# A two-layer hybrid encoder: softmax sums applied to a pair of heads' result, and five smaller moves around attention

## The chip, the cores and the metric

The kernel runs on one core of a Trainium2 chip. The metric is the device time of one execution in microseconds (us). The core's engines run side by side, each through its own list of instructions in order: TensorE (PE; its weight loads are listed as PEld), VectorE (DVE), ScalarE (ACT), GpSimd (POOL) and SyncE (SP), which only issues transfers. POOL and ACT can issue transfers too.

## The reference

Two layers on x of 512 x 1024, each a feed-forward half step, a mixer, and another feed-forward half step. All inputs are float32. The mixer, cut to what matters here:

```python
proj = h @ w_in
qa, ka, va, ub, qc, kc, vc, f_lin, g_lin = split(proj)
ya = chunked_relpos_attention(qa, ka, va, qk_gain[0], qk_gain[1], rel_bias)   # 8 heads of 64
yb = multiscale_pool(ub, w_pool, pool_scale)
yc = forgetting_attention(qc, kc, vc, qk_gain[2], qk_gain[3], f_lin + forget_bias)
branch = einsum('bsnw,nwd->bsnd', stack([ya, yb, yc]), w_branch)
merged = sum(sigmoid(g_lin) * branch)
return merged @ w_out

# in both attentions, with q and k normalised per head (rms_norm):
logits = q @ k.T + bias          # a: bias by relative distance; c: cq - ck, the cumulated log gates
p = softmax(where(mask, logits, -1e30))
out = p @ v
```

## The kernel before

Every product is made of three float32r products, hi x hi, hi x lo and lo x hi (`triple`, lines 119 to 121). For that each operand is split into a high and a low half: weights in `wchunk` (line 271 on ACT makes `whi`, line 273 on DVE makes `wlo`), other data in `split_to` (lines 378 and 379). Weights stream in on SP's queue.

The program is written to a scheduler that puts each engine's instructions in order by a model of its own. On top of it the code keeps a counter, `pe[0]`, of the matmul work issued so far in units of one 512-column matmul. `later(delay, fn)` defers a piece of work until the counter has gone on by `delay`: a row block's transposes come LAG_T = 24 units after its logits, a head's value products LAG_V = 14 units after the transposes. Between the heads, `attention` draws work from a generator, the filler, so that PE has projections or merge products to do while the other engines work through a softmax.

A mixer goes through these stages: the projections of q and k for attention "a" (`proj_qk` 0 and 1) and of v (`proj_v` 2); attention "a" over eight heads, with the projections for attention "c" (3, 4, 5) and the forgetting gates (`forget`) as filler; attention "c" over eight heads, with the first merge (`merge_units` of `ya`) as filler; then pooling, the other merges and the output product. In layer 0 the two attentions lie at about 465 to 700 us, in layer 1 at about 1690 to 1900 us.

One row block (128 queries) of one head in `attention`: logits on PE (L951, L952), the bias strip added and the row maximum taken on DVE (L955), Exp with its row sum on ACT (L959), the reciprocal of the sum on DVE (L961), the probabilities scaled by it (L962, on POOL for the first three blocks and on DVE for the fourth), transposes on PE (L974), which ACT and DVE copy out of PSUM as a high and a low half (L978, L979). A half of a head's value products (L996, L997) goes to a PSUM tile `o`. ACT copies one half of it (L1000), DVE adds the other (L1001), and ACT and POOL split the 64 x 256 result into a pair's rows `y` (L378, L379). A pair is two heads, 128 rows. `merge_units` reads the pair's rows as right operand k of its products.

PSUM has eight banks: four under the name `acc` (projections and merges) and four under `mm` (logits, transposes, value products, the turning of q and k). A projection's evacuation copies the bank to `ptb` (L826), squares the bank's content (L828) and sums the squares (L829). The first projection of a mixer starts from normalised data that comes in two halves of 256 tokens (`norm.back`), with three weight chunks loaded ahead (`pre`) and the fourth loaded after both halves. The turning of q and k (L844 to L859) is deferred in steps set by TURN.

Of the kernel before, what the change touches and what calls it, by code (L numbers as in the profile page):

```python
# [40 lines left out]
def encoder_kernel(tc, xT, c, w_ada, b_ada, gains, w_gate, w_up, w_down, w_qkv, w_f, w_ubg,  # L41
# [130 lines left out]

    x_dram = dr.tile([4, P, 2 * T], F32, name="x_dram")
    fv_dram = [dr.tile([H, FVLEN], F32, name=f"fv_dram{l}") for l in range(L)]

    last = {}

# [591 lines left out]
    def proj(l, col, evac, pre=None, norm=None):  # L769
        accs = [acc() for _ in range(NT)]  # L770

        def three(t, k, hi, lo):
            tk = slice(t * P, (t + 1) * P)
            triple2(accs[t], hhi[:, k, tk], hlo[:, k, tk], hi, lo, k == 0, k == KD - 1)

        if norm is not None:
            for hs in range(2):
                norm.back(hs, mmt)
                if hs == 0:
                    later(FRONT2, lambda: norm.front(1, mmt))  # L780
                    later(BACK2, lambda: norm.back(1, mmt))
                for k in range(6):
                    hi, lo = pre[k // 2]
                    for t in (2 * hs, 2 * hs + 1):
                        three(t, k, hi[:, k % 2, :], lo[:, k % 2, :])
        else:
            for c in range(2):
                hi, lo = qkv_chunk(l, col, c)
                for kk in range(2):
                    for t in range(NT):  # L790
                        three(t, 2 * c + kk, hi[:, kk, :], lo[:, kk, :])
                        yield
        held = [(c, *qkv_chunk(l, col, c)) for c in ((3,) if pre else (2, 3))]
        for t in range(NT):
            for c, hi, lo in held:
                for kk in range(2):
                    three(t, 2 * c + kk, hi[:, kk, :], lo[:, kk, :])
                    yield
            evac(t, accs[t])
# [18 lines left out]
    def proj_qk(l, col, gcol, is_q, res, pre=None, norm=None):  # L818
# [3 lines left out]
        def evac(t, a):  # L822
# [2 lines left out]
            qn, ss = qs  # L825
            nc.scalar.copy(qn[:, t, :], a)  # L826
            sq = t2(T)
            nc.scalar.activation(sq, a, AF.Square)  # L828
            nc.vector.tensor_reduce(ss[:, t, :], sq.rearrange("p (h d) -> p h d", h=H), axis=AX.X, op=ALU.add)  # L829

        yield from proj(l, col, evac, pre, norm)
# [44 lines left out]

    turns = []
    heads = [H]
    TURN = 52
    Q_GATE, K_GATE = (2, 2, 4, 4), (6, 6, 8, 8)  # L880

    def finish_turns(upto=3):
# [57 lines left out]
    def attention(qs, ks, vs, strip, ys, filler, budget, group):  # L940


        open_pt = {}

        def logits(h, i, strips):
            p, off = divmod(h, 2)
# [8 lines left out]
            nc.vector.tensor_tensor_reduce(out=lg, in0=s[:, :n], in1=strips[i], scale=-1.0, scalar=BIG,  # L955
                                           op0=ALU.add, op1=ALU.min, accum_out=mx)
            pr = t2(T)[:, :n]
            sm = st([P, 1], F32, "sm", 4)
            nc.scalar.activation(pr, lg, AF.Exp, bias=mx, scale=-1.0, accum_out=sm)  # L959
            rs = st([P, 1], F32, "rs", 4)  # L960
            nc.vector.reciprocal(rs, sm)  # L961
            (nc.vector if i == NT - 1 else nc.gpsimd).tensor_scalar(pr, pr, rs, None, op0=ALU.mult)  # L962
            pe[0] += 0.5 * (i + 1.5)
            later(LAG_T, lambda: turn(h, i, pr), group)

# [18 lines left out]
        def weigh(h, half, pt):  # L984
# [1 line left out]
            rows = slice(off * HD, off * HD + HD)  # L986
            other = slice(HD - off * HD, 2 * HD - off * HD)
            if off == 0 and half == 0:
                ys.append(blk("b"))
            y = ys[p]  # L990
            o = mmt((P, HALF))
            nj = 2 * half + 2
            for j in range(nj):
                q0 = P if j == nj - 1 else 0
# [3 lines left out]
            cols = slice(half * HALF, (half + 1) * HALF)  # L998
            yl = t1(T)[:, :HALF]
            nc.scalar.copy(yl[rows, :], o[other, :])  # L1000
            nc.vector.tensor_tensor(yl[rows, :], o[rows, :], yl[rows, :], op=ALU.add)  # L1001
            split_to(y[rows, 0, cols], y[rows, 1, cols], yl[rows, :], nc.gpsimd)
            pe[0] += 1.0 * nj

        for h in range(H):
            strips = strip(h)
# [13 lines left out]
            for _ in filler:  # L1020
                pass

    LAG_T, LAG_V = 24, 14


    def pool_front(l, g):
# [77 lines left out]
    class Mixer:  # L1104
# [10 lines left out]
        def run(self, nxt):  # L1115
# [14 lines left out]
            def fill_a():  # L1130
                yield from proj_qk(l, 3, g8[:, 2:3], True, qc)
                yield from proj_qk(l, 4, g[:, 3:4], False, kc)
                yield from proj_v(l, 5, "v2", vc)
                yield from forget(l)

            lo_share[0] = LO_SHARE
            attention(qa, ka, va, lambda h: strip_a(l, h), ya, fill_a(), FILL_A, "a")
# [133 lines left out]
```

## Time and profile before

| what | value |
|---|---|
| median of 3 runs | 2451.54 us (2450.65 to 2452.75) |
| profiled execution | 2450.88 us |
| its span | 2448.9 us |
| granted TensorE clock, mean | 0.998 |
| DMA packets, bytes | 116279, 320.23 MB |

The span is the time from the first to the last recorded instruction; 2.0 us of the execution lie outside it. In the rows of the profile, "mm L974 <- POOL t L962" under the waits means that line 974 with its output `mm` waited until POOL's line 962 had written `t`; names carry no buffer numbers. `t` stands for the work tiles `t1` and `t2`, `b` for the tiles of 128 x 1024 that hold y and q.

### The profile page before, as it was taken

How to read it: one execution, taken by the hardware profiler on the slowest of the kernel's cores; microseconds unless marked ns; L12 is line 12 of the kernel's file. 1: busy time of each engine (PE TensorE's matmuls, PEld its weight loads, DVE VectorE, ACT ScalarE, POOL GpSimd, SP SyncE). 2: the span in 40 equal slices, each digit the busy share in tenths (PEclk: the TensorE clock that was granted, in tenths of full speed). 3: DMA queues.
4: the chain of work that ended last, by engine and by line, in shares of the span. 5: the costliest groups of instructions: out<-in, count | busy, mean ns of one | idle time of the engine just before them, and what ended most of it. 6: DMA issues, size and time to landing. Idle time of an engine off the chain costs nothing. (4 is left out here: it accounts for less than half of the span.)

```text
span 2448.9 us, 34028 instructions
## 1 busy us (share of the span) xinstructions
PE 2396.8 (98%) x12966; PEld 2051.8 (84%) x12966; DVE 1600.5 (65%) x2859; ACT 1110.3 (45%) x1888; POOL 377.3 (15%) x439
## 2 busy tenths in 40 slices
PE   7999999999999999999999999999999999999999
PEld 5798888777888898988898888878777888988888
DVE  8978766677643378787678656477765434765463
ACT  5333345677642353333453334366765333533341
POOL 3000002144532110000000000123354322000000
PEclk9999999999999999999999999999999999999999
DMA  7756543222323426565327423223133234233232
GB/s 284 251 170 209 198 147 113 78 82 88 116 91 103 142 75 240 174 206 198 129 85 243 138 86 121 103 90 96 61 109 99 95 111 139 87 104 112 67 114 78
DMA packets 116279, 320.23 MB, mean 131 GB/s; under 512 B 11122, under 2 KB 13298, under 8 KB 116116
## 3 DMA queue, kind: packets, MB, share of 16 engines
q1 hardware_dynamic: 114962, 313.86, 38.3%
q0 software_dynamic: 1152, 4.19, 0.4%
q8 instruction: 102, 1.67, 0.3%
q14 instruction: 61, 0.50, 0.1%
q10 hardware_dynamic: 2, 0.00, 0.0%
HBM read 311.64 MB, written 6.38 MB: 130 GB/s over the span
## 5 line engine op out<-in xcount | busy, mean ns | idle before, releaser
L271 ACT CAST whi<-raw 128x1024 fp32r<-128x1024 f32 (+1 forms) x325 | 338.2, 1044 | 595.1 <-PE mm L120 289.2
L273 DVE TENSOR_TENSOR wlo<-raw,whi 128x1024 fp32r<-128x1024 f32 x317 | 392.2, 1240 | 197.4 <-ACT whi L271 194.2
L121 PE MATMUL mm<-hhi,wlo 128*128 128x512 f32 x744 | 289.8, 390 | 0.7 <-DVE wlo L273 0.4
L119 PE MATMUL mm<-hhi,whi 128*128 128x512 f32 x744 | 290.2, 390 | 0.0
L120 PE MATMUL mm<-hlo,whi 128*128 128x512 f32 x744 | 290.0, 390 | 0.0
L119 PE MATMUL acc<-b,whi 128*128 128x512 f32 (+1 forms) x704 | 264.1, 376 | 1.7 <-ACT b L378 1.7
L121 PE MATMUL acc<-b,wlo 128*128 128x512 f32 (+1 forms) x704 | 262.1, 374 | 3.5 <-DVE wlo L273 3.5
L120 PE MATMUL acc<-b,whi 128*128 128x512 f32 (+1 forms) x704 | 262.4, 373 | 0.0
L197 DVE CUSTOM_DVE_ANT_0 v<-v,b,badac 128x1024 f32<-128x1024 f32 x144 | 188.3, 1316 | 60.9 <-DMA v<-in_w_ada_dram 60.7
L119 PE MATMUL acc<-hhi,whi 128*128 128x512 f32 x480 | 190.7, 399 | 1.7 <-ACT hhi L738 1.7
L121 PE MATMUL acc<-hhi,wlo 128*128 128x512 f32 x480 | 188.9, 394 | 0.0
L120 PE MATMUL acc<-hlo,whi 128*128 128x512 f32 x480 | 188.5, 393 | 0.2 <-DVE hlo L741 0.2
L121 PEld LDWEIGHTS mm<-hhi,wlo 128*128 128x128 f32 x744 | 139.7, 188 | 30.9 <-DVE wlo L273 1.6
L119 PEld LDWEIGHTS mm<-hhi,whi 128*128 128x128 f32 x744 | 140.0, 188 | 27.9
L120 PEld LDWEIGHTS mm<-hlo,whi 128*128 128x128 f32 x744 | 139.7, 188 | 27.4
L121 PEld LDWEIGHTS acc<-b,wlo 128*128 128x128 f32 x704 | 133.8, 190 | 27.2 <-DVE wlo L273 4.6
L119 PEld LDWEIGHTS acc<-b,whi 128*128 128x128 f32 x704 | 133.3, 190 | 23.8 <-ACT b L378 2.6
L120 PEld LDWEIGHTS acc<-b,whi 128*128 128x128 f32 x704 | 133.3, 189 | 23.2 <-DVE b L379 0.9
L119 PE MATMUL acc<-whi,hhi 128*128 128x512 f32 x336 | 137.7, 411 | 4.4 <-ACT t L828 3.7
L120 PE MATMUL mm<-b,whi 128*128 128x512 f32 (+1 forms) x384 | 135.8, 354 | 0.0
L119 PE MATMUL mm<-b,whi 128*128 128x512 f32 (+1 forms) x384 | 135.8, 354 | 0.0
L121 PE MATMUL mm<-b,wlo 128*128 128x512 f32 (+1 forms) x384 | 135.6, 354 | 0.0
(300 smaller groups left out, 5598.3 us busy)
## 6 DMA issues: line engine op xcount, KB each, us to landing
v<-in_w_ada_dram SPq DMA_DIRECT2D x144, 512.0 KB, 4.4
raw<-in_w_down_dram SPq DMA_DIRECT2D x88, 512.0 KB, 3.5
raw<-in_w_up_dram SPq DMA_DIRECT2D x82, 512.0 KB, 3.4
b<-in_w_gate_dram SPq DMA_DIRECT2D x76, 512.0 KB, 5.3
raw<-in_w_ubg_dram SPq DMA_DIRECT2D x56, 512.0 KB, 3.3
raw<-in_w_qkv_dram SPq DMA_DIRECT2D x42, 512.0 KB, 3.7
raw<-in_w_branch_dram SPq DMA_DIRECT2D x24, 512.0 KB, 3.6
raw<-in_w_out_dram SPq DMA_DIRECT2D x16, 512.0 KB, 3.3
```

Source lines behind the costliest of these rows:

```text
L119: mm(o, lh, rh, start=start, stop=False, skip_group_check=onto)
L120: mm(o, lh, rl, start=False, stop=False, skip_group_check=onto)
L121: mm(o, ll, rh, start=False, stop=stop, skip_group_check=onto)
L197: dot = nc.vector.tensor_tensor_reduce(out=raw, in0=raw, in1=silc[0], scale=1.0, scalar=badac[:, l, j, d:d + 1], op0=ALU.mult, op1=ALU.add ...
L271: nc.scalar.copy(hi, raw)
L273: lo_eng.tensor_tensor(lo, raw, hi.bitcast(F32), op=ALU.subtract)
```

## The change

- The reciprocal and the scaling of each row block go. The row sums of a pair (two heads, four blocks each) are gathered in a tile of 128 x 8, one reciprocal is taken for the pair, and a transfer on POOL's queue writes it to `inv_dram` as 1024 single floats. A new `norm_rows`, LAG_N = 8 units after the pair's last value product, reads them back as two broadcast transfers of 64 x 512 on POOL's queue; DVE multiplies the pair's unscaled 128 x 512 rows by them, and ACT and DVE split the result. The splits by quarter (64 x 256, ACT and POOL) go.
- The Square of a projection reads the copy in SBUF in place of the PSUM bank.
- The value products of attention "c" go to an `acc` bank.
- `forget` stands ahead of `proj_v` 5 in the filler.
- The first projection loads its fourth weight chunk after its first half, and finishes two of four token blocks in each half.
- TURN is 60 in place of 52.

```diff
@@ -172,6 +172,7 @@
 
     x_dram = dr.tile([4, P, 2 * T], F32, name="x_dram")
     fv_dram = [dr.tile([H, FVLEN], F32, name=f"fv_dram{l}") for l in range(L)]
+    inv_dram = {(g, p): dr.tile([2, T], F32, name=f"inv_dram_{g}{p}") for g in "ac" for p in range(4)}
 
     last = {}
 
@@ -783,6 +784,13 @@
                     hi, lo = pre[k // 2]
                     for t in (2 * hs, 2 * hs + 1):
                         three(t, k, hi[:, k % 2, :], lo[:, k % 2, :])
+                if hs == 0:
+                    end = qkv_chunk(l, col, 3)
+                for t in (2 * hs, 2 * hs + 1):
+                    for kk in range(2):
+                        three(t, 6 + kk, end[0][:, kk, :], end[1][:, kk, :])
+                    evac(t, accs[t])
+            return
         else:
             for c in range(2):
                 hi, lo = qkv_chunk(l, col, c)
@@ -790,7 +798,7 @@
                     for t in range(NT):
                         three(t, 2 * c + kk, hi[:, kk, :], lo[:, kk, :])
                         yield
-        held = [(c, *qkv_chunk(l, col, c)) for c in ((3,) if pre else (2, 3))]
+        held = [(c, *qkv_chunk(l, col, c)) for c in (2, 3)]
         for t in range(NT):
             for c, hi, lo in held:
                 for kk in range(2):
@@ -825,7 +833,7 @@
             qn, ss = qs
             nc.scalar.copy(qn[:, t, :], a)
             sq = t2(T)
-            nc.scalar.activation(sq, a, AF.Square)
+            nc.scalar.activation(sq, qn[:, t, :], AF.Square)
             nc.vector.tensor_reduce(ss[:, t, :], sq.rearrange("p (h d) -> p h d", h=H), axis=AX.X, op=ALU.add)
 
         yield from proj(l, col, evac, pre, norm)
@@ -876,7 +884,7 @@
 
     turns = []
     heads = [H]
-    TURN = 52
+    TURN = 60
     Q_GATE, K_GATE = (2, 2, 4, 4), (6, 6, 8, 8)
 
     def finish_turns(upto=3):
@@ -941,6 +949,7 @@
 
 
         open_pt = {}
+        sums, rows_of = {}, {}
 
         def logits(h, i, strips):
             p, off = divmod(h, 2)
@@ -955,11 +964,14 @@
             nc.vector.tensor_tensor_reduce(out=lg, in0=s[:, :n], in1=strips[i], scale=-1.0, scalar=BIG,
                                            op0=ALU.add, op1=ALU.min, accum_out=mx)
             pr = t2(T)[:, :n]
-            sm = st([P, 1], F32, "sm", 4)
-            nc.scalar.activation(pr, lg, AF.Exp, bias=mx, scale=-1.0, accum_out=sm)
-            rs = st([P, 1], F32, "rs", 4)
-            nc.vector.reciprocal(rs, sm)
-            (nc.vector if i == NT - 1 else nc.gpsimd).tensor_scalar(pr, pr, rs, None, op0=ALU.mult)
+            if odd == 0 and i == 0:
+                sums[p] = st([P, 2 * NT], F32, "sm", 3)
+            nc.scalar.activation(pr, lg, AF.Exp, bias=mx, scale=-1.0,
+                                 accum_out=sums[p][:, odd * NT + i:odd * NT + i + 1])
+            if odd and i == NT - 1:
+                rs = st([P, 2 * NT], F32, "rs", 2)
+                nc.vector.reciprocal(rs, sums[p])
+                nc.gpsimd.dma_start(inv_dram[group, p].rearrange("h (i q) -> q (h i)", q=P), rs)
             pe[0] += 0.5 * (i + 1.5)
             later(LAG_T, lambda: turn(h, i, pr), group)
 
@@ -986,9 +998,9 @@
             rows = slice(off * HD, off * HD + HD)
             other = slice(HD - off * HD, 2 * HD - off * HD)
             if off == 0 and half == 0:
-                ys.append(blk("b"))
-            y = ys[p]
-            o = mmt((P, HALF))
+                rows_of[p] = st([P, T], F32, "b", NB)
+            y = rows_of[p]
+            o = (acc if group == "c" else mmt)((P, HALF))
             nj = 2 * half + 2
             for j in range(nj):
                 q0 = P if j == nj - 1 else 0
@@ -998,9 +1010,20 @@
             cols = slice(half * HALF, (half + 1) * HALF)
             yl = t1(T)[:, :HALF]
             nc.scalar.copy(yl[rows, :], o[other, :])
-            nc.vector.tensor_tensor(yl[rows, :], o[rows, :], yl[rows, :], op=ALU.add)
-            split_to(y[rows, 0, cols], y[rows, 1, cols], yl[rows, :], nc.gpsimd)
+            nc.vector.tensor_tensor(y[rows, cols], o[rows, :], yl[rows, :], op=ALU.add)
             pe[0] += 1.0 * nj
+            if off and half:
+                later(LAG_N, lambda: norm_rows(p), group)
+
+        def norm_rows(p):
+            rb = t2(T)
+            for z in range(2):
+                nc.gpsimd.dma_start(rb[z * HD:(z + 1) * HD, :], inv_dram[group, p][z:z + 1, :].broadcast_to([HD, T]))
+            y = blk("b")
+            ys.append(y)
+            full = rows_of[p]
+            nc.vector.tensor_tensor(full, full, rb, op=ALU.mult)
+            split_to(y[:, 0, :], y[:, 1, :], full)
 
         for h in range(H):
             strips = strip(h)
@@ -1020,7 +1043,7 @@
             for _ in filler:
                 pass
 
-    LAG_T, LAG_V = 24, 14
+    LAG_T, LAG_V, LAG_N = 24, 14, 8
 
 
     def pool_front(l, g):
@@ -1130,8 +1153,8 @@
             def fill_a():
                 yield from proj_qk(l, 3, g8[:, 2:3], True, qc)
                 yield from proj_qk(l, 4, g[:, 3:4], False, kc)
+                yield from forget(l)
                 yield from proj_v(l, 5, "v2", vc)
-                yield from forget(l)
 
             lo_share[0] = LO_SHARE
             attention(qa, ka, va, lambda h: strip_a(l, h), ya, fill_a(), FILL_A, "a")
```

Counted over the whole program, PE and SP issue as many instructions as before. DVE has 128 reciprocals of 128x1 and 32 scalings of 128x512 less, and 16 reciprocals of 128x8, 16 multiplications and 16 subtractions of 128x512 more. ACT has 64 casts of 64x256 less and 16 of 128x512 more. POOL has 96 scalings and 64 subtractions less, and 16 writes and 32 reads more.

POOL, before, in attention "c" of layer 0 (`strip` and `ssum` are the bias strips of a head, `cmask` the causal mask, `rs` the reciprocals, `b` a pair's rows):

```order
L379 TENSOR_TENSOR b_1099_5589<-t1_1101_5595,b_1099_5589 64x256
L937 TENSOR_TENSOR ssum_1103_5605<-ssum_1103_5605,cmask_112 128x128
L962 TENSOR_SCALAR t2_1113_5638<-t2_1113_5638,rs_1115_5641 128x256
L962 TENSOR_SCALAR t2_1120_5666<-t2_1120_5666,rs_1122_5669 128x384
L937 TENSOR_TENSOR strip_1186_5898<-strip_1186_5898,cmask_112 128x128 x3
L379 TENSOR_TENSOR b_1099_5589<-t1_1128_5695,b_1099_5589 64x256
L937 TENSOR_TENSOR ssum_1142_5743<-ssum_1142_5743,cmask_112 128x128
L962 TENSOR_SCALAR t2_1146_5755<-t2_1146_5755,rs_1148_5758 128x128
L379 TENSOR_TENSOR b_1099_5589<-t1_1150_5769,b_1099_5589 64x256
```

POOL, after, at the first pair of "c" (in brackets the semaphores that the instruction waits for; DMASW are transfers of POOL's queue, DMAHW those of SP's):

```order
L974 DMA inv_dram_c0_127<-rs_1076_5588 128x8x1 [waits DMASW0_49,DVE_49]
L945 TENSOR_TENSOR ssum_1080_5609<-ssum_1080_5609,cmask_112 128x128 [waits DMAHW2_49,Pool_49]
L945 TENSOR_TENSOR strip_1156_5888<-strip_1156_5888,cmask_112 128x128 [waits DMAHW4_49,DVE_49]
...
L1021 DMA t2_1115_5732<-inv_dram_c0_127 64x512 [waits DMASW1_49,DMASW6_49,DMASW0_49,DMASW7_49,PE_49,Activation_49]
L1021 DMA t2_1115_5732<-inv_dram_c0_127 64x512
L945 TENSOR_TENSOR ssum_1120_5754<-ssum_1120_5754,cmask_112 128x128 [waits DMAHW6_49,DVE_49]
L945 TENSOR_TENSOR strip_1196_6033<-strip_1196_6033,cmask_112 128x128 [waits DMAHW7_49,DVE_49]
...
L974 DMA inv_dram_c1_128<-rs_1153_5869 128x8x1 [waits DMASW3_49,DVE_49]
```

The scalings and splits are gone; the read of `inv_dram` waits for its write and for the last users of its tile, and the mask additions of the following heads stand behind it.

DVE, before, in the same attention:

```order
L961 RECIPROCAL rs_1163_5803<-sm_1162_5801 128x1
L979 TENSOR_TENSOR pta_1171_5834<-mm_1172_5835,pta_1171_5834 128x128
L961 RECIPROCAL rs_1170_5831<-sm_1169_5829 128x1
L1001 TENSOR_TENSOR t1_1174_5854<-mm_1173_5845,t1_1174_5854 64x256
L955 ISA t1_1177_5870,mx_1178_5871<-mm_1176_5867,ssum_1142_5743 128x512
L955 ISA mx_1178_5871 128x1
L979 TENSOR_TENSOR pta_1171_5834<-mm_1175_5862,pta_1171_5834 128x2x128
...
L961 RECIPROCAL rs_1181_5876<-sm_1180_5874 128x1
L962 TENSOR_SCALAR t2_1179_5873<-t2_1179_5873,rs_1181_5876 128x512
L979 TENSOR_TENSOR ptb_1184_5891<-mm_1185_5892,ptb_1184_5891 128x3x128
```

DVE, after, around the multiplication of the first pair of "c" (line 1025; `b_1042` the pair's rows, `t2_1115` the broadcast reciprocals):

```order
L964 ISA t1_1112_5724,mx_1113_5725<-mm_1111_5721,ssum_1080_5609 128x512 [waits DVE_49,DMAHW2_49,PE_49,Pool_49]
...
L1168 SCALAR_TENSOR_TENSOR xv_1125_5768<-t1_1106_5698,acc_1107_5700 128x512 [waits PE_49]
L964 ISA t1_1122_5763,mx_1123_5764<-mm_1121_5760,strip_1119_5752 128x128 [waits DMAHW1_49,PE_49,Activation_49]
...
L991 TENSOR_TENSOR ptb_1117_5745<-mm_1118_5746,ptb_1117_5745 128x3x128 [waits Activation_49]
L1025 TENSOR_TENSOR b_1042_5462<-b_1042_5462,t2_1115_5732 128x512 [waits DMASW2_49,DMASW1_49]
L1013 TENSOR_TENSOR b_1130_5780<-acc_1131_5781,t1_1132_5786 64x256 [waits Activation_49]
L964 ISA t1_1134_5798,mx_1135_5799<-mm_1133_5795,strip_1119_5752 128x256 [waits DVE_49,PE_49]
...
L380 TENSOR_TENSOR b_1116_5735<-b_1042_5462,b_1116_5735 128x512 [waits Activation_49]
L991 TENSOR_TENSOR ptb_1117_5745<-mm_1137_5806,ptb_1117_5745 128x4x128 [waits Activation_49]
```

The reciprocals (L961) and the scaling (L962) of the row blocks are gone, and the multiplication, which waits for the reads, stands between a copy of transposes and the row maximum of a later block (line 964, formerly 955).

PE, before, at the step from "a" to "c" of layer 0, where the first merge product reads the last pair of "a" (`b_1010`):

```order
L951 MATMUL mm_1104_5611<-b_961_5107,b_805_4550 128x128 [waits DVE_49]
L952 MATMUL mm_1104_5611<-b_961_5107,b_806_4551 128x128
L951 MATMUL mm_1110_5632<-b_961_5107,b_805_4550 128x256 [waits DVE_49]
L952 MATMUL mm_1110_5632<-b_961_5107,b_806_4551 128x256
L119 MATMUL acc_1124_5674<-b_1010_5311,whi_1049_5402 128x512 [waits Activation_49]
L120 MATMUL acc_1124_5674<-b_1010_5311,whi_1049_5402 128x512 [waits Pool_49]
L121 MATMUL acc_1124_5674<-b_1010_5311,wlo_1050_5403 128x512
...
L974 MATMUL mm_1116_5647<-ident_66,t2_1090_5563 128x128 [waits DVE_49,PE_49]
```

PE, after, at the same place (`b_1037` is the last pair's rows; lines 960 and 986 are the logits and transposes):

```order
L960 MATMUL mm_1060_5536<-b_931_5064,b_793_4536 128x384 [waits DVE_49]
L961 MATMUL mm_1060_5536<-b_931_5064,b_794_4537 128x384
L986 MATMUL mm_1065_5545<-ident_66,t2_1050_5491 128x128 [waits DVE_49,Activation_49]
L119 MATMUL acc_1058_5522<-b_961_5200,whi_1002_5310 128x512
...
L119 MATMUL acc_1058_5522<-b_1037_5444,whi_1002_5310 128x512 [waits Activation_49]
L120 MATMUL acc_1058_5522<-b_1037_5444,whi_1002_5310 128x512 [waits DVE_49]
L121 MATMUL acc_1058_5522<-b_1037_5444,wlo_1003_5311 128x512
...
L960 MATMUL mm_1072_5580<-b_931_5064,b_793_4536 128x512 [waits DVE_49]
```

The product of the last pair stood behind the second logits of the second head of "c" and waited for ACT and POOL; now it waits for ACT and DVE, and stands directly behind the product of the pair before it. The transposes no longer wait for POOL.

## The prediction

> **What bounds the kernel now.** I read the busy shares first, then a table by stage, then the list of waits, then the operations that the change touches. In the first rows, the columns are busy time, share of the span and number of instructions.
>
> ```profile
> span 2448.9 us, 34028 instructions
> PE 2396.8 (98%) x12966; PEld 2051.8 (84%) x12966; DVE 1600.5 (65%) x2859; ACT 1110.3 (45%) x1888; POOL 377.3 (15%) x439
> ...
> core 0: us, PE busy (x) PEld busy (x) DVE busy (x) ACT busy (x) POOL busy (x), PEclk, DMA share, GB/s
> ...
> 410.00:700.00 290.00, 276.70 (x1415) 223.83 (x1414) 199.84 (x481) 191.08 (x406) 115.85 (x153) 0.99 0.30 92
> 700.00:1610.00 910.00, 909.03 (x5096) 796.99 (x5095) 596.35 (x968) 359.90 (x541) 67.92 (x63) 1.00 0.42 143
> 1610.00:1900.00 290.00, 275.05 (x1408) 221.17 (x1407) 199.44 (x478) 190.41 (x404) 113.25 (x148) 1.00 0.30 91
> ...
> 520.00:620.00 100.00, 91.42 (x478) 71.41 (x477) 75.14 (x197) 70.11 (x163) 45.01 (x62) 0.98 0.29 89
> ```
>
> TensorE (PE) is the bound everywhere: 98% busy, and in the 910 us between the two mixers it stands idle for under 1 us. The only place where other engines cost time is the attention stages, 410 to 700 us (layer 0) and 1610 to 1900 us (layer 1). There PE is idle for 290 - 276.70 = 13.3 us and 290 - 275.05 = 14.9 us. The change issues exactly as many matmuls as before, so it can win only from these 28 us, of which 8.6 us lie between 520 and 620 us, around the step from attention "a" to "c". What PE and its weight loads (PEld) wait for, in columns total us, times, longest:
>
> ```profile
> PEld mm L974 <- POOL t L962: 14.0, 20, 1.1
> PE mm L974 <- POOL t L962: 6.8, 15, 0.7
> PEld acc L119 <- ACT t L828: 6.6, 8, 1.7
> PEld mm L951 <- DVE t L1001: 6.5, 6, 1.5
> PE mm L951 <- DVE t L1001: 4.6, 6, 1.1
> PEld mm L951 <- DVE ptb L979: 4.2, 4, 1.9
> PE acc L119 <- ACT t L828: 3.7, 6, 1.3
> PEld mm L951 <- DVE mx L955: 3.6, 6, 0.8
> ```
>
> A wait shows up twice, once before the weight load and once before the matmul behind it, so the true loss lies between the PE row and the PEld row. The largest is the transposes (L974) waiting until POOL has scaled the probabilities (L962). The rest are full PSUM banks: a bank that the Square (L828) still reads, and one that the value add (L1001) or the copies of transposes (L979) have not yet emptied.
>
> **The change, part by part.** The operations concerned, as busy us, mean ns | idle before:
>
> ```profile
> L962 POOL TENSOR_SCALAR t<-t,rs 128x128 f32<-128x128 f32 (+2 forms) x96 | 88.7, 927 | 138.2 <-DVE rs L961 117.7 <-PE acc L121 5.7 <-PE mm L974 5.7
> L962 DVE TENSOR_SCALAR t<-t,rs 128x512 f32<-128x512 f32 x32 | 16.6, 520 | 1.2
> L961 DVE RECIPROCAL rs<-sm 128x1 f32<-128x1 f32 x128 | 20.2, 159 | 37.7 <-ACT t L959 37.6
> L379 POOL TENSOR_TENSOR b<-t,b 64x256 fp32r<-64x256 f32 x64 | 56.4, 882 | 94.5 <-ACT b L378 93.4
> L378 ACT CAST b<-t 64x256 fp32r<-64x256 f32 x64 | 25.9, 404 | 26.7 <-DVE t L1001 26.3
> L379 DVE TENSOR_TENSOR b<-b,b 128x512 fp32r<-128x512 f32 x14 | 9.1, 681 | 0.0
> L378 ACT CAST b<-b 128x512 fp32r<-128x512 f32 x14 | 8.2, 622 | 0.7 <-DVE b L499 0.7
> ```
>
> *Scaling out of the chain (part 1).* Today a row block goes Exp, reciprocal (0.16 us), scaling (0.93 us on POOL for three blocks of four, 0.52 us on DVE for the fourth), transposes. Afterwards the transposes read the Exp's output. The chain is 0.93 + 0.16 = 1.1 us shorter, as long as the longest wait of its row (1.1). So this wait can go whole: between 6.8 and 14.0 us over both layers. I take 10, the middle, since what is late next is near: the same PE stretch also waits for emptied banks (L1001, L979), and a bank wait that was hidden behind the scaling comes out. The reciprocals that stand in the way on DVE for the fourth blocks count 1 us more (bounds 0 and 1.1, one wait's length).
>
> In work, POOL loses 88.7 + 56.4 = 145 us. DVE loses 20.2 + 16.6 = 36.8 and gains 16 reciprocals of 128x8 (nearest row 0.16, so 2.6), 16 multiplies and 16 subtractions of 128x512 (nearest row 0.68 each, so 21.8): 12 us less. ACT loses 25.9 and gains 16 x 0.62 = 10: 16 us less. None of this is on PE; the lighter DVE and ACT can shorten the bank waits "L951 <- ptb L979" and "<- mx L955". Of their 4.2 + 3.6 us I take 1.5; bounds 0 and 7.8.
>
> *The new end of a pair.* The normalised rows now come after multiply, cast and subtraction: 0.68 + 0.62 + 0.68 = 2.0 us in a row, against 0.40 + 0.88 = 1.3 us today. Who waits: the merge products of that pair. Seven pairs of eight in a layer have their product much later. The last pair of "a" has its product (k = 3) as the first filler of "c", a few matmuls behind. There PE can stand 0.7 us (the difference) to 2.0 us (all of it) per layer; I take 1.3, so +2.5 in all. This hits the worst stretch, 520 to 620 us.
>
> *The way through DRAM.* Sixteen writes of 128x8 floats and 32 broadcast reads go on POOL's queue. The nearest transfers of POOL's queue are the eight 512 KB stores of x:
>
> ```profile
> L1119 POOL DMA_DIRECT2D x_dram<-xv x8: 573/573/762, 365.9 to 1596.4; - x8
> ...
> DMA to landing us min/median/max: 2.9/3.2/4.2
> ```
> ```profile
> q0 software_dynamic: 1152, 4.19, 0.4%
> ```
>
> They take 0.57 us of POOL each and land in 3.2 us, with 1152 / 8 = 144 packets each. The write has 1024 single elements. At the same issue time the round trip is 0.57 + 3.2 + 2 x 0.57 + 3.2 = 8.1 us; if issuing goes with the packets, the write takes 0.573 x 1024 / 144 = 4.1 us and the trip 11.6 us (both estimates from these rows). How long the kernel gives it, from pair 0 of "a" (start, duration):
>
> ```profile
> 487.46 0.16 DVE L961 RECIPROCAL rs<-sm 128x1 f32<-128x1 f32 x1 [0.94 <-ACT t L959]
> ...
> 499.65 0.43 DVE L1001 TENSOR_TENSOR t<-mm,t 64x256 f32<-64x256 f32 x1
> ```
>
> The first is the pair's last reciprocal, the second its last value add, 12.6 us from end to end. The new multiply is deferred by 8 more matmul units (LAG_N), and a unit is 0.23 us, as the starts of the matmuls in the fence below show: 12.6 + 1.8 = 14.4 us. The trip fits either way, with 2.8 us to spare in the worse case. I charge +1 us for places where it does not. The upper end: 16 waits of 1 us on DVE, all reaching PE, +16. Queued behind the read on POOL are the mask adds for later heads' strips (L937; four a head), and on DVE behind the multiply the row maxima of the next heads. POOL, with 145 us less to do, is the cover for its own queue; SP gets no new transfer.
>
> The Trainium skill, "SBUF — State Buffer", section "A bandwidth-pool intuition that's wrong (but worth ruling out)", says that descriptors of transfers from GpSimd's queue cannot be written while a VectorE operation holds the port pair the two engines share, so that a transfer of some 0.6 us took 3.1 us. By that the worse trip would be some 2.5 us longer per transfer and would just miss its place. The eight stores show 573 to 762 ns of issue and no landing above 4.2 us, with DVE 65% busy; so the trace does not bear it out, though only eight cases can speak.
>
> *Square from SBUF (part 2).* The accumulator bank is free after the copy (L826), not after the Square.
>
> ```profile
> 437.13 0.39 PE L121 MATMUL acc<-whi,hlo 128*128 128x512 f32 x1
> 437.67 0.59 ACT L826 COPY ptb<-acc 128x512 f32<-128x512 f32 x1
> 438.15 0.60 ACT L828 ACTIVATE t<-acc 128x512 f32<-128x512 f32 x1
> 438.81 0.50 PE L119 MATMUL acc<-whi,hhi 128*128 128x512 f32 x1 [1.29 <-ACT t L828]
> 439.15 0.40 PE L120 MATMUL acc<-wlo,hhi 128*128 128x512 f32 x1
> 439.39 0.40 PE L121 MATMUL acc<-whi,hlo 128*128 128x512 f32 x1
> 439.62 0.40 PE L119 MATMUL acc<-whi,hhi 128*128 128x512 f32 x1
> ```
>
> The longest wait of its row sits here. The copy ends at 438.26 and the Square at 438.75, so 0.5 us goes. What is left comes from the copy itself, which starts late in ACT's queue behind the turns of q. One such wait per layer, 2 x 0.5 = 1.0, and the four short waits that make up 3.7 - 2 x 1.3 = 1.1 us go whole: 2.1 us on PE; by the PEld row up to 4.0. I take 2. That Square now waits for the copy's write costs ACT some tenths; ACT is 45% busy.
>
> *Other banks in "c" (part 3).* Logits and value products no longer share banks there. "L951 <- L1001" is 4.6 to 6.5 us, and in "a" the sharing stays; I take 1, bounds 4.6 gained, or the same lost if the merge products, which use the four acc banks too, now wait.
>
> *Gates earlier (part 4).* Two table loads and a serial chain per layer move ahead of the v projection:
>
> ```profile
> L959 ACT ACT_TABLE_LOAD x1 | 1.3, 1283 | 0.0
> ...
> L909 DVE SCALAR_TENSOR_TENSOR t<-t,t 8x512 f32<-8x512 f32 x1 | 0.7, 680 | 1.5 <-ACT t L908 1.5
> ```
>
> Today DVE stands there for 1.5 us right before "c" starts, and the strips of "c" are loaded after it. Moved up, it lies beside projection work of PE. I take 0.75 per layer, half that wait: 1.5; bounds 0 and 3. Should its new place not cover it, the logits of a later head of "a" stand as long, and it costs the same 3 us.
>
> *First projection in halves, TURN 60 (parts 5, 6).*
>
> ```profile
> 403.44 2.36 DVE L273 TENSOR_TENSOR wlo<-raw,whi 128x1024 fp32r<-128x1024 f32 x2 [0.45 <-ACT whi L271]
> ...
> 407.73 0.59 ACT L826 COPY ptb<-acc 128x512 f32<-128x512 f32 x1 [3.38 <-PE acc L121]
> ```
>
> Nothing: the first projection's evacuation waits for PE and not PE for it, the last weight half is split by 405.8 us, about when PE would now come to it, and the turns move by 8 units (1.8 us), beside PE's projection work. If that cover goes, a wait like the 1.29 us above per layer: plus or minus 2.6.
>
> Sum: -10 - 1 - 1.5 + 2.5 + 1 - 2 - 1 - 1.5 = -13.5 us. The profiled execution took 2450.88 us (span 2448.9 and 2.0 around it), 0.7 below the median of 2451.54; from the median it gives 2438 us. The ends: every gain at its upper bound (14.0 + 1.1 + 7.8 + 4.0 + 4.6 + 3) overlaps itself, and all idle time of the two stages is 28 us, so about -27; with scaling at 6.8, the bank gain lost and the DRAM trip at a third of its upper end, about 0.
>
> **The rivals.** *No change:* the waits only move. PE would wait for the emptied banks where it now waits for the scaling, since in "a" logits, transposes and value products still share the mm banks. For it: four of the eight waits above are bank waits, and a transpose that runs earlier only reaches the next full bank earlier. Against it: those banks are emptied by DVE and ACT, which both get lighter. Time: 2447 to 2455 us.
>
> *Slower:* the trip through DRAM. It decides from 14.4 us on: each microsecond above holds DVE, in order, with the row maxima behind it, and PE has only 24 units (5.5 us) between logits and transposes, which it uses already. At 17 us it is 2.6 us for each of 16 pairs, 42 us, less 13.5 gained: +28, so 2480 us; at 15.5 us it is already +4. For it: 1024 elements, against 144 packets in the only stores of this queue that the trace shows. Against it: the estimate of 11.6 us. The Trainium skill, "DMA: Bandwidth & Descriptors", section "Rules for kernel authors", warns that a last dimension that is not contiguous becomes one descriptor per element; that is this write, and the trace has no such transfer to judge it.
>
> *Larger gain:* the PEld rows are the true ones: scaling 14.0 and 1.1, Square 4.0, banks 6.5, gates 3 make 28.6, as much as PE's whole idle time in both stages; at 27 us less it gives 2424 us. For it: 8.6 of layer 0's 13.3 us lie at the step from "a" to "c", which three of the parts touch. Against it: "a" keeps its banks, and the copy at 438 us stays late.
>
> **How the numbers follow.** Forecast (5 to 22 us less) 0.66; larger gain 0.08; no change 0.15; slower 0.11. A measurement of this kernel tells 0.2%, 4.9 us, from nothing. Faster is 0.66 + 0.08 = 0.74, same 0.15, slower 0.11. The range, 2424 to 2453, holds the first three but for their edges. The likeliest case alone would be 2430 to 2446.
>
> **What would show it.** PE idle in 410 to 700 us down from 13.3 to 6 or 7. No wait of the transposes for POOL; if one for the Exp (L959) of several us takes its place, part 1 was oversized. The wait for L828 gone but for some 0.8 us at 438 us. A wait of the merge product for the subtraction at 580 us of 1 to 2 us. The multiply's idle time for its reads under 1 us a pair: if it is 2 us or more, the slower rival is right in its mechanism and the forecast wrong.

## The result, and the profile after

The changed kernel takes 2516.51 us (median of 4 runs, 2515.22 to 2520.04) against 2452.14 us before: a ratio of 1.0264, with a 95% interval of 1.0246 to 1.0282. It is 64 us slower where 13.5 us less was forecast. The profiled execution spans 2515.4 us. First its page, with the columns as before:

```profile
span 2515.4 us, 33638 instructions
PE 2421.9 (96%) x12966; PEld 2071.3 (82%) x12966; DVE 1593.7 (63%) x2747; ACT 1094.8 (44%) x1840; POOL 259.7 (10%) x327
...
q0 software_dynamic: 3200, 8.46, 1.3%
```

POOL, DVE and ACT are all less busy, as the change meant. The same number of matmuls counts as 25 us more busy time, and PE's idle time grew by 41 us; together they are the 66 us by which the span grew. Where it grew, by stage (start:end, length, then the engines' busy time, and behind POOL's the granted clock, the DMA engines' busy share and GB/s):

```profile
410.00:520.00 110.00, 104.72 (x502) 85.10 (x500) 72.50 (x143) 68.81 (x126) 18.86 (x26) 0.97 0.33 87
520.00:580.00 60.00, 53.73 (x274) 41.99 (x275) 46.67 (x108) 42.01 (x90) 10.59 (x17) 0.97 0.29 80
580.00:720.00 140.00, 120.28 (x593) 98.63 (x592) 68.68 (x160) 64.33 (x154) 21.61 (x44) 0.89 0.38 87
...
1800.00:1960.00 160.00, 141.21 (x725) 115.60 (x724) 86.79 (x205) 80.61 (x194) 27.29 (x57) 0.95 0.38 91
```

The last two stretches in the kernel before:

```profile
580.00:720.00 140.00, 135.78 (x700) 111.54 (x698) 84.47 (x214) 80.75 (x184) 73.64 (x102) 0.99 0.32 104
...
1800.00:1960.00 160.00, 155.35 (x768) 126.98 (x767) 86.00 (x197) 78.97 (x169) 72.25 (x94) 1.00 0.30 98
```

Attention "c" is hit: PE idles 19.7 us of 140 in layer 0 and 18.8 of 160 in layer 1, where it idled 4.2 and 4.7 before, and the clock falls to 0.89 and 0.95. The waits show what for (total us, times, longest):

```profile
DVE b L1025 <- DMA t<-inv_dram_c: 65.6, 8, 14.1
...
POOL strip L945 <- DMA strip<-fv_dram: 123.7, 15, 15.7
...
DVE b L1025 <- DMA t<-inv_dram_a: 19.8, 5, 7.7
...
PE acc L1008 <- ACT ptb L990: 21.0, 8, 5.8
PE acc L119 <- ACT b L379: 12.8, 3, 6.4
...
PE mm L986 <- ACT t L969: 4.6, 5, 1.8
...
PE acc L119 <- ACT ptb L834: 3.0, 4, 0.9
```

The transposes' wait for the scaling is gone, and 4.6 us of wait for the Exp take its place. But DVE stands 85 us at the new multiplication (L1025), 8.2 us on average at the eight in "c" (14.1 at most), and PE waits behind it for the copies of transposes (ptb) and for the normalised rows (b). The reads are late, and so are the strips for "c". The transfers (KB each, median us from issue to landing), and the new write by itself:

```profile
strip<-fv_dram SPq DMA_DIRECT2D x16, 384.0 KB, 5.3
...
ssum<-fv_dram SPq DMA_DIRECT2D x16, 256.0 KB, 7.1
...
t<-inv_dram_a POOLq DMA_DIRECT2D x16, 128.0 KB, 3.4
t<-inv_dram_c POOLq DMA_DIRECT2D x16, 128.0 KB, 3.9
...
inv_dram_a<-rs POOLq DMA_DIRECT2D x8, 4.0 KB, 10.4
inv_dram_c<-rs POOLq DMA_DIRECT2D x8, 4.0 KB, 11.0
```
```profile
L974 POOL DMA_DIRECT2D inv_dram_c<-rs x8: 915/917/927, 616.1 to 1946.3; - x8
...
DMA to landing us min/median/max: 9.6/10.5/12.0
```

Issuing the 1024 floats costs POOL 0.92 us only, but they land after 10.5 us. One pair of "c" as the engines lived through it (start, duration; idle time in brackets), from the timelines of POOL, SP, DVE and PE:

```profile
616.08 0.92 POOL L974 DMA_DIRECT2D inv_dram_c<-rs  x1 [1.88 <-DVE mx L964]
...
633.14 1.30 POOL L945 TENSOR_TENSOR strip<-strip,cmask 128x128 f32<-128x128 f32 x3 [15.65 <-DMA strip<-fv_dram]
634.38 1.05 POOL L1021 DMA_DIRECT2D t<-inv_dram_c  x2
...
621.77 0.32 SPq L939 DMA_DIRECT2D strip<-fv_dram  x1
...
637.86 0.69 DVE L1025 TENSOR_TENSOR b<-b,t 128x512 f32<-128x512 f32 x1 [9.43 <-DMA t<-inv_dram_c]
...
634.30 0.40 PE L121 MATMUL acc<-hhi,wlo 128*128 128x512 f32 x1
640.52 0.58 PE L1008 MATMUL acc<-ptb,v 128*128 128x256 f32 x1 [5.82 <-ACT ptb L990]
...
646.32 0.63 PE L121 MATMUL acc<-b,wlo 128*128 128x512 f32 x1
...
647.34 0.40 PE L121 MATMUL acc<-b,wlo 128*128 128x512 f32 x1
```

The write starts at 616.1 and lands 10.9 us later. A strip load that SP issues at 621.8 lets POOL go on only at 633.1, after 11.4 us. POOL's reads stand behind that strip's mask additions and leave at 634.4, though the write has landed by then. DVE gets its rows at 637.9, with everything queued behind the multiplication held. From the start of the write to the multiplication it is 21.8 us. PE loses 5.8 us, and after the gap a 512-column matmul takes 0.63 us, until 646.7; then 0.40 again. The granted clock (the number behind POOL's) is 0.50 meanwhile:

```profile
636.50:637.00 0.50, 0.00 (x0) 0.00 (x0) 0.00 (x0) 0.00 (x0) 0.00 (x0) 0.78 0.54 156
...
644.00:646.00 2.00, 2.00 (x7) 1.52 (x6) 1.88 (x4) 0.92 (x3) 0.76 (x2) 0.50 0.14 43
...
647.00:647.50 0.50, 0.50 (x3) 0.41 (x3) 0.12 (x1) 0.35 (x2) 0.00 (x0) 0.98 1.01 393
```

So this hold is paid for twice. The Trainium skill, "TensorE: Matmul & The Clock Gate", section "Part 1: The HAM clock gate (the \"warmup\" mystery)", has PE at half rate after at least one idle window of some 3.4 us, until at least one such window has been busy. This trace has the half rate too, but sooner: the clock drops 2.1 us after PE stops (634.7 to 636.8), and it is full again 6.5 us after PE goes on (640.5 to 647.0), which the rule allows.

What the DMA engines do meanwhile, in stretches of 2 us:

```profile
616.00:618.00 2.00, 2.00 (x13) 1.72 (x12) 1.97 (x3) 1.06 (x4) 1.39 (x2) 1.00 0.25 2
618.00:620.00 2.00, 2.00 (x14) 1.69 (x13) 0.44 (x3) 1.17 (x3) 0.00 (x0) 1.00 0.85 82
620.00:622.00 2.00, 2.00 (x11) 1.68 (x10) 1.46 (x4) 0.45 (x3) 0.00 (x0) 1.00 0.46 23
622.00:624.00 2.00, 2.00 (x14) 1.80 (x13) 0.47 (x1) 2.00 (x4) 0.00 (x0) 1.00 0.79 33
624.00:626.00 2.00, 2.00 (x12) 1.62 (x11) 1.94 (x4) 0.74 (x2) 0.00 (x0) 1.00 0.60 20
626.00:628.00 2.00, 2.00 (x13) 1.72 (x12) 1.24 (x6) 1.33 (x4) 0.00 (x0) 1.00 0.31 18
...
630.00:632.00 2.00, 2.00 (x14) 1.69 (x13) 0.00 (x0) 0.00 (x0) 0.00 (x0) 1.00 1.02 399
```

From 620 to 626, while the floats are on the way, the engines count as 46 to 79% busy and move only 20 to 33 GB/s, with a 512 KB weight load (issued at 617.1) and the strip waiting; in the 2 us before it was 82 GB/s. Behind the floats it is 399. The busy share is counted roughly, as the 1.02 shows.

### The profile page after: what moved, and what is told of

Its sections match the earlier page's. It is cut to its first block, busy times and chain, and to the rows that moved or that the text cites. A ratio compares the mean times of both kernels' runs of the same rounds, so it can differ in the third digit from the quotient of the medians.

```text
span 2515.4 us, 33638 instructions
## 1 busy us (share of the span) xinstructions
PE 2421.9 (96%) x12966; PEld 2071.3 (82%) x12966; DVE 1593.7 (63%) x2747; ACT 1094.8 (44%) x1840; POOL 259.7 (10%) x327
## 5 line engine op out<-in xcount | busy, mean ns | idle before, releaser
L119 PE MATMUL acc<-b,whi 128*128 128x512 f32 (+1 forms) x704 | 266.2, 379 | 12.9 <-ACT b L379 12.8
```

The source lines that it names most:

```text
L119: mm(o, lh, rh, start=start, stop=False, skip_group_check=onto)
```

## The experiments

Each time stands against runs of the kernel before on the same chip; ratios carry their 95% intervals. Differences between two kernels are those of their medians. Some pairs ran at different times or on different chips, where the kernel before took 2448.75 to 2452.14 us, so that such a difference can be off by some 3 us.

**Which part costs.** Part 1 undone in the changed kernel, its other five moves kept:

```diff
-                nc.vector.reciprocal(rs, sums[p])
-                nc.gpsimd.dma_start(inv_dram[group, p].rearrange("h (i q) -> q (h i)", q=P), rs)
...
-                later(LAG_N, lambda: norm_rows(p), group)
...
+            rs = st([P, 1], F32, "rs", 4)
+            nc.vector.reciprocal(rs, sm)
+            (nc.vector if i == NT - 1 else nc.gpsimd).tensor_scalar(pr, pr, rs, None, op0=ALU.mult)
```

> The changed kernel with part 1 undone: the row blocks are scaled one by one again, the other five moves stay. Theory: part 1 carries the whole loss of 64 us, and the other moves are worth what the forecast said (2 + 1 + 1.5): 2447 us, between 2440 and 2452. Rival: the loss in attention "c" comes from the gates or from the acc banks of the value products: then it stays, 2490 us or more.

2462.53 us, 1.0051 (1.0034 to 1.0068): neither. Without part 1 the loss of 64 us is gone, but the other moves are no gain either: by themselves they cost some 14 us. The reverse, the same lines put into the kernel before:

```diff
-            nc.vector.reciprocal(rs, sm)
...
+                nc.vector.reciprocal(rs, sums[p])
+                nc.gpsimd.dma_start(inv_dram[group, p].rearrange("h (i q) -> q (h i)", q=P), rs)
...
+                later(LAG_N, lambda: norm_rows(p), group)
```

> The kernel before with part 1 alone. Theory (part 1 carries the loss): 2505 to 2525 us, with the multiplications in "c" waiting 5 us or more each for the broadcast reads. Rival (the loss comes from the other moves): about 2440 us.

2520.30 us, 1.0289 (1.0270 to 1.0307). Part 1 carries the loss.

**The write or the reads.** The changed kernel, its reads from a constant tensor and the write left out:

```diff
-                nc.gpsimd.dma_start(inv_dram[group, p].rearrange("h (i q) -> q (h i)", q=P), rs)
-                nc.gpsimd.dma_start(rb[z * HD:(z + 1) * HD, :], inv_dram[group, p][z:z + 1, :].broadcast_to([HD, T]))
+                nc.gpsimd.dma_start(rb[z * HD:(z + 1) * HD, :], one_dram[z:z + 1, :].broadcast_to([HD, T]))
```

> The changed kernel without the sixteen writes of the reciprocals; the reads take their rows from a constant DRAM tensor that is written once at the start, so the output is not scaled by the row sums. Theory A (the write of 1024 single floats is what costs, by its landing of 10.5 us and by what it does to the transfers beside it): 2435 to 2445 us. Theory B (the reads are late because they stand in POOL's order behind mask additions that wait for strips, whatever the write does): 2495 us or more, with DVE still waiting 5 to 9 us at each multiplication of "c".

2435.07 us, 0.9939 (0.9924 to 0.9954): theory A. This kernel leaves the writes out. Sixteen writes of 4 KB cost 81 us (2516.5 - 2435.1). Stages of this kernel, in the columns used above:

```profile
520.00:580.00 60.00, 56.26 (x286) 43.77 (x285) 49.65 (x110) 42.79 (x92) 8.42 (x16) 0.97 0.31 98
580.00:720.00 140.00, 138.70 (x720) 115.94 (x719) 83.45 (x183) 74.95 (x167) 34.87 (x61) 1.00 0.35 114
...
1800.00:1960.00 160.00, 158.72 (x781) 132.51 (x780) 82.48 (x159) 71.28 (x142) 38.01 (x60) 1.00 0.33 107
```

PE's idle time of 19.7 us in "c" of layer 0 is down to 1.3. Next, the same 4 KB in long runs:

```diff
-                nc.gpsimd.dma_start(inv_dram[group, p].rearrange("h (i q) -> q (h i)", q=P), rs)
...
+            nc.tensor.transpose(tr[:2 * NT, :P], rs, ident)      # 28 units later
+            nc.scalar.copy(rt, tr[:2 * NT, :P])
+            nc.gpsimd.dma_start(inv_dram[group, p].rearrange("h (i q) -> (h i) q", q=P), rt)
```

> The changed kernel with the reciprocals transposed on PE first and written as eight rows of 512 bytes; the round trip through DRAM stays. Theory A (single floats are the cause): the write lands in 2 to 4 us and the time is 2440 to 2455 us. If the round trip as such is the cause, or POOL's order (theory B): 2490 us or more.

2441.55 us, 0.9966 (0.9954 to 0.9979): theory A again. The transfers in this kernel:

```profile
strip<-fv_dram SPq DMA_DIRECT2D x16, 384.0 KB, 3.5
...
inv_dram_a<-t POOLq DMA_DIRECT2D x8, 4.0 KB, 2.4
inv_dram_c<-t POOLq DMA_DIRECT2D x8, 4.0 KB, 1.9
```

The write lands in 2 us and the strips are back at 3.5. POOL's queue counts 3200 packets in both kernels, so their number does not show the difference. The eight rows also come from 8 partitions in place of 128, and leave later; no run separates this from the length of the runs. That 128 partitions alone are slow is unlikely, since the stores of x come from 128 and land in 3.1 us in the changed kernel.

**Its landing or what it does to others.** The floats are written, but the reads take the constant tensor and wait for none of them:

```diff
-                nc.gpsimd.dma_start(rb[z * HD:(z + 1) * HD, :], inv_dram[group, p][z:z + 1, :].broadcast_to([HD, T]))
+                nc.gpsimd.dma_start(rb[z * HD:(z + 1) * HD, :], one_dram[z:z + 1, :].broadcast_to([HD, T]))
```

> The changed kernel with its sixteen writes of single floats, but the reads take a constant DRAM tensor written once at the start and so wait for no write; the output is not scaled by the row sums. Theory A1 (the loss is the wait for the write's landing): as without the write, 2433 to 2440 us. Theory A2 (the write also slows the transfers beside it: strips for "c" land in 5.3 us, 3.5 with the eight-row write): it keeps a part of the loss, 2450 to 2490 us, with strip landings as long as in the changed kernel.

2494.22 us, 1.0172 (1.0155 to 1.0189): theory A2. 59 of the 81 us (2494 - 2435) remain although no instruction waits for the write; the other 22 come with the wait for its landing. Beside a write (611.9) a strip load of SP still takes 10.4 us until POOL can go on:

```profile
617.56 0.32 SPq L941 DMA_DIRECT2D strip<-fv_dram  x1
...
628.00 1.30 POOL L947 TENSOR_TENSOR strip<-strip,cmask 128x128 f32<-128x128 f32 x3 [14.72 <-DMA strip<-fv_dram]
```

Without the writes POOL goes on 3.3 to 3.7 us after such a load. DVE's idle time at the multiplication is 47.4 us here and 17.3 us without the write:

```profile
  DMA t<-one_dram: 47.4, 9
```
```profile
  DMA t<-one_dram: 17.3, 8
```

The same, with the reads on SP's queue, past the mask additions:

```diff
-                nc.gpsimd.dma_start(rb[z * HD:(z + 1) * HD, :], one_dram[z:z + 1, :].broadcast_to([HD, T]))
+                nc.sync.dma_start(rb[z * HD:(z + 1) * HD, :], one_dram[z:z + 1, :].broadcast_to([HD, T]))
```

> As the kernel that writes single floats and reads constant rows (2494 us), with the two reads of a pair issued on SP's queue in place of POOL's, so that they no longer stand behind the mask additions there; the output is not scaled by the row sums. Theory C (the writes delay the strips, and the reads are late because they stand behind the strips' mask additions): most of the 59 us goes, 2435 to 2455 us. Theory D (the late strips and slowed transfers suffice by themselves): 2475 us or more.

2497.22 us, 1.0189 (1.0172 to 1.0207): theory D; theory C falls. POOL's order alone is not what makes the reads late. Issued from another queue, past the mask additions and without a wait for the write, they are slow themselves: 6.9 us in the median, up to 10.4, for 128 KB. The same reads on SP's queue beside eight-row writes (the third kernel under "A better version") land in 3.9 us, 4.0 at most, so it is the floats that make the difference. The two lines:

```profile
DMA to landing us min/median/max: 3.9/6.9/10.4
```
```profile
DMA to landing us min/median/max: 3.0/3.9/4.0
```

Half of the floats (512 a write, reads constant and on POOL's queue):

```diff
-                nc.gpsimd.dma_start(inv_dram[group, p].rearrange("h (i q) -> q (h i)", q=P), rs)
+                nc.gpsimd.dma_start(inv_dram[group, p][0:1].rearrange("h (i q) -> q (h i)", q=P), rs[:, :NT])
```

> As the kernel that writes single floats and reads constant rows on POOL's queue (2494 us), with half of the floats: each write takes the first head's 128x4 alone; the output is not scaled by the row sums. Theory (the cost goes with the number of single floats): the write lands in some 5 to 6 us, and the time lies well below the middle of 2435 and 2494, 2440 to 2465 us, since the strips have some slack. If a write costs by its fixed part: 2485 us or more.

2479.01 us, 1.0125 (1.0108 to 1.0142): between the two. The write still lands only after 8.9 us, so most of its length does not go with the number of floats; the loss does in part (44 us in place of 59). I had expected 5 to 6 us and 2440 to 2465.

```profile
DMA to landing us min/median/max: 8.3/8.9/9.8
```

**Parts 2 to 6.** Without part 1 they cost 14 us; taken back one after the other. Gates at their old place:

```diff
-                yield from forget(l)
                 yield from proj_v(l, 5, "v2", vc)
+                yield from forget(l)
```

> The changed kernel with part 1 undone and the gates back behind the v projection: parts 2, 3, 5 and 6 alone. Theory (the gates' chain on DVE and ACT delays reciprocals and scaling where it now lies, a PE wait of 5.6 us for the scaling in each layer, and this is the 14 us of the kernel without part 1): 2443 to 2449 us. Rival (the banks or the Square cost it): 2458 us or more.

2460.09 us, 1.0034 (1.0021 to 1.0047). My theory falls. In the kernel with the early gates PE's longest wait is for the scaling,

```profile
PEld mm L983 <- POOL t L971: 28.8, 23, 6.0
```

and with the gates back its row reads 10.9 us with 1.0 at most, yet the time hardly changes. The row lost 18 us and the whole 2.4, which the intervals do not tell from nothing. Value products back in mm banks, too:

```diff
-            o = (acc if group == "c" else mmt)((P, HALF))
+            o = mmt((P, HALF))
```

> Parts 2, 5 and 6 alone: part 1 undone, gates at the old place, value products of "c" back in mm banks. Theory (the acc banks cost the 9 to 14 us of the kernel without part 1): 2446 to 2451 us. If Square, halves or TURN cost it: 2457 to 2463 us.

2455.20 us, 1.0017 (1.0008 to 1.0027): between my two ranges. It is 4.9 us less than with the acc banks, but the intervals overlap. Gates and banks together cost 8 us (1.0051 against 1.0017, with intervals apart), though neither step is clear of the noise by itself. Then Square alone, and Square with TURN 60:

```diff
-            nc.scalar.activation(sq, a, AF.Square)
+            nc.scalar.activation(sq, qn[:, t, :], AF.Square)
```

> The kernel before with part 2 alone. By the forecast 2 us less, within what can be told (2446 to 2452 us), with the waits for the Square replaced by shorter ones for the copy. If another order of the instructions follows from it: 2455 us or more.

```diff
-    TURN = 52
+    TURN = 60
```

> The kernel before with parts 2 and 6 alone (Square from SBUF, TURN 60). Parts 2, 5 and 6 together gave 4 us more than before. If TURN costs them: 2452 to 2458 us. If the halves of the first projection cost them: 2446 to 2451 us.

2448.26 us, 0.9987 (0.9978 to 0.9996), and 2454.06 us, 1.0018 (1.0009 to 1.0028). Square gives 3 us; TURN 60 beside it costs 7.6 (0.0031 of 2450), and the halves add nothing to that that could be told. Why 1.8 us more between turns cost so much was not tried further.

**A better version.** Part 1 in the kernel before with the eight-row write, reads on POOL's queue, which is this line and the transpose and copy shown above:

```diff
+            nc.gpsimd.dma_start(inv_dram[group, p].rearrange("h (i q) -> (h i) q", q=P), rt)
```

> The kernel before with part 1 alone, and its write made as eight rows. If the parts simply add up, with parts 2 to 6 at +14: 2441 - 14 = 2427 us. If parts 2 to 6 are harmful only beside the scaling and worth a little (4.5 us) without it: 2444 to 2448 us.

2439.56 us, 0.9951 (0.9936 to 0.9966): below what I gave for parts 2 to 6 worth a little, above what adding up gives. With part 1 in place they make no difference that can be told (2441.55 with them). No way through DRAM at all, the broadcast made by PE in the changed kernel:

```diff
+            for m, z in ((P, 1), (HD, 0)):
+                for i in range(NT):
+                    c = z * NT + i
+                    nc.tensor.transpose(rb[:m, i * P:(i + 1) * P], iv[:, c:c + 1].broadcast_to([P, m]), ident)
```

> The changed kernel without any way through DRAM: PE transposes the reciprocals, each column broadcast, straight into an mm bank, eight transposes a pair, and DVE multiplies from there. 128 transposes more on PE at some 0.1 us each are 10 to 13 us: 2445 to 2450 us against 2435 without the write. If the four mm banks are too few for it: 2455 us or more.

2442.42 us, 0.9963 (0.9948 to 0.9977), below the 2445 to 2450 that I gave: DVE waits 0.6 us in all for these rows, but the 128 transposes take 16.6 us of PE, the engine that is the bound. Then the eight-row write with the reads on SP's queue, in the kernel before:

```diff
-                nc.gpsimd.dma_start(rb[z * HD:(z + 1) * HD, :], inv_dram[group, p][z:z + 1, :].broadcast_to([HD, T]))
+                nc.sync.dma_start(rb[z * HD:(z + 1) * HD, :], inv_dram[group, p][z:z + 1, :].broadcast_to([HD, T]))
```

> The kernel before with part 1 alone, the write as eight rows, and the reads on SP's queue. DVE waits 18 us in all for the reads when they come from POOL's queue; if that order is what makes them late, these waits go and the time falls below 2439.6 us by a few us (2433 to 2438). If SP's queue holds them behind weights instead: 2440 to 2450 us.

2432.85 us, 0.9924 (0.9909 to 0.9939): 18 us faster than before. The interval hardly overlaps that of the reads on POOL's queue, so once the floats no longer block the engines the queue of the reads seems to count; DVE's idle time at the multiplications of "c" falls from 13.6 to 10.1 us.

```profile
  DMA t<-inv_dram_c: 10.1, 8
```

Square and early gates on top:

```diff
+            nc.scalar.activation(sq, qn[:, t, :], AF.Square)
...
+                yield from forget(l)
                 yield from proj_v(l, 5, "v2", vc)
```

> Part 1 with the write as eight rows and the reads on SP's queue (2432.9 us), with Square from SBUF (part 2) and the gates ahead of the v projection (part 4). By the forecast's terms 2 + 1.5 us less: 2428 to 2431 us. If gains of Square and gates are used up already, or another order of the instructions costs as much: 2433 to 2440 us.

2431.73 us, 0.9926 (0.9911 to 0.9941): the same as without them, between my two ranges. Both beat the kernel before and the changed one.

## Why the prediction was wrong

*What bounds the kernel* was right, and taking the scaling out of the chain is a gain. Without the write the changed kernel is 13.7 us faster than before; forecast were 13.5. That the sum fits is partly luck: it holds parts 2 to 6, for which I took 4.5 us and which give nothing that can be told beside part 1, so part 1 is worth more than its terms. They come to 9 us (10 + 1 + 1.5 - 2.5 - 1), and part 1 alone with the eight-row write gives 12. Eighteen us with a good path for the reciprocals are within the upper ends I had for scaling and bank waits. The wait for the Exp, my sign for an oversized part 1, did appear (4.6 us), but it does not come from part 1 by itself: with part 1 alone and the eight-row write it is 0.2 us in all.

*The way through DRAM* is the step that failed, in two places. I took the landing of the write, 3.2 us, from the nearest row of its queue, the stores of x, and let only the issue grow with the elements (0.57 to 4.1 us). It was the reverse: the issue stayed at 0.92 us, and the landing went to 10.5. By these medians the trip is 0.92 + 10.5 + 1.06 + 3.6 = 16.1 us in place of 8.1 to 11.6, past the 14.4 us from which the slower rival decides (the 12.6 us in it are 12.5 from end to end, 500.08 - 487.62, which changes nothing). That rival had the right wait: DVE's idle time at the multiplication, 85 us over 16 pairs, or 5.3 a pair, is above the 2 us a pair that was to show it; it got 0.11. Its price was too low: at 16.1 us its rule gives 16 x 1.7 - 13.5 = 14 us lost, not 64, in part because the reads also stood behind the late strips (21.8 us in the pair shown). The row the trip was judged by had long runs, the new transfer has runs of four bytes, and I named that row the nearest.

Second, I asked only who waits for the write. 59 of its 81 us remain when nothing waits for it; what is left are transfers that are slower beside it: strips of "c" and the reads, which share the 16 engines. "SP gets no new transfer" was true and proved nothing. The upper end that I charged, 16 us for 16 DVE waits, left this out, and it also left out that PE comes back from a gap at a lower clock (0.50, with 0.63 us a matmul against 0.40).

*The two rules that I weighed.* The Trainium skill, "DMA: Bandwidth & Descriptors", section "Rules for kernel authors", which I had set against this write, was right in its advice: with the last dimension contiguous the loss is gone. The other, that of the Trainium skill, "SBUF — State Buffer", section "A bandwidth-pool intuition that's wrong (but worth ruling out)", on descriptors held up by VectorE, does not show in the reads, which land in 3.6 us in the median, nor in the eight-row write, which lands in 1.9. Whether it has a part in the 10.5 us of the single floats no run here shows.

*Terms of the smaller parts.* Square: 2 forecast, 3 measured. The wait for it is gone, and the longest wait for the copy (L834) that takes its place is 0.9 us, about the 0.8 expected, though these waits add up to 3.0 us, against 3.7 for the Square before. Banks in "c": 1 forecast as a gain; without part 1, they and the gates together lose 8. Gates: 1.5 forecast as a gain; no gain in any pair of runs. TURN: 0 forecast, 7.6 lost beside the old scaling; the "plus or minus 2.6" there was too narrow. The merge products did wait for normalised rows, 12.8 us in three waits of up to 6.4 where I had 2.5, since the rows come after the late multiplication.

*The rivals "no change" and "larger gain"* rest on bank waits; neither happened.

## What to carry to other kernels

Price a small transfer by its contiguous runs and not by its bytes, and take the price from a row with runs of that length; where there is none, the landing is as unknown as the issue. Ask of a new transfer not only who waits for it, but what else is on the DMA engines while it drains. Where a small vector must cross partitions through DRAM, a transpose on PE that makes its rows contiguous costs 16 transposes and 16 copies here and turns a loss of 64 us into a gain of 7 to 12, or of 18 with the reads on SP's queue.

## What the runs showed of the hardware that was not expected

Sixteen writes of 4 KB in four-byte runs land in 10.5 us in the median, and the same bytes in eight rows of 512 bytes in 1.9; half the floats still take 8.9. While they drain, transfers of SP's queue crawl: in the pair shown the engines count as 46 to 79% busy at 20 to 33 GB/s from 620 to 626 us, and a strip load of 384 KB holds POOL until 11.4 us after its issue, where landings of 3.5 are the median beside eight-row writes. Why the length hardly goes with the number of floats stays open. After the first write of the changed kernel, issued at 487.1 and landed 10.4 us later, the engines count as idle from 489 to 493; by this rough count, a part of the time is not the moving of data.

```profile
489.00:491.00 2.00, 2.00 (x12) 1.65 (x12) 1.88 (x6) 1.90 (x4) 0.00 (x0) 1.00 0.00 0
491.00:493.00 2.00, 2.00 (x12) 1.66 (x11) 2.00 (x4) 1.12 (x4) 0.00 (x0) 1.00 0.00 0
```

Whether single floats behave the same on SP's queue was not tried.
